# Mixer B's values leave PSUM through ScalarE alone, inverse roots in eight operations, and the first head's transposes behind a gate's matmuls

## The chip, the core and the metric

The kernel runs on one core of one Trainium2 chip. A core has TensorE (PE in the profile), VectorE (DVE), ScalarE (ACT), GpSimd (POOL) and SyncE (SP, which only issues DMAs). The metric is the device time of one execution in microseconds (us); smaller is better.

## The reference

Two layers of an encoder trunk on x of 512 tokens by 1024 channels, all in float32. Each layer has two attention branches whose outputs are gated, added and projected, and then a feed-forward part with a short convolution. The part of one layer that matters here:

```python
h = rms_norm(x, norm_mix[l])
z = h @ w_in[l]
qa, ka, va, qi, ki, wi, cq, ckv, kr, ga, gb = split_cols(z)
y_a = sparse_indexed_attention(qa, ka, va, qi, ki, wi, rel_bias, topk)  # topk = 128

cq = rms_norm(cq, b_cq_norm[l])                      # 384 wide
qb = (cq @ b_w_uq[l]).reshape(B, S, 8, 96)           # 64 plain + 32 rotated
ckv = rms_norm(ckv, b_ckv_norm[l])                   # 256 wide
kv = (ckv @ b_w_ukv[l]).reshape(B, S, 8, 64 + 64)    # keys | values
kb = concat([kv[..., :64], k_rope]);  vb = kv[..., 64:]
qb = rms_norm(qb, b_q_norm[l]);  kb = rms_norm(kb, b_k_norm[l])
y_b = latent_attention(qb, kb, vb)                   # 8 heads, softmax, chunk mask

merged = sigmoid(ga + ..) * (y_a @ w_proj_a[l]) + sigmoid(gb + ..) * (y_b @ w_proj_b[l])
x = x + merged @ w_out[l]
```

`rms_norm` is x times the inverse square root of mean(x²) + 1e-6, times a gain.

## The kernel before

**Matmuls.** Every float32 operand is split into a high part (`..h`, rounded) and a low part (`..l`, the rest), and each product is three matmuls (high·high, low·high, high·low) that add up in one PSUM bank of 128 x 512. A weight arrives by DMA as `wr`; ScalarE casts it to `wh`; and `wl` = `wr` − `wh` comes either from VectorE, or from ScalarE and a DMA that GpSimd issues. PSUM has eight banks: two `D` (dense products), three `L` (small products and scores), two `T` (transposes), one `Y` (attention outputs).

**Order of a layer.** Norm, index scores of mixer A, the latent rows, the gate columns `gb` m = 0 to 3; then `attn_b(0)` and `attn_b(1)`, which make keys, queries and values of heads 0 to 3 and 4 to 7; then mixer B head by head; then mixer A, the output projections, and the feed-forward part. What is dense (`gb` m = 4 to 7, gate A, projections) is written as a `Filler` from which a `Feeder` takes a step now and then, so that TensorE has matmuls between the steps of the heads. `top_k` (16 rounds, on VectorE alone, of three `MAX` and three `MATCH_REPLACE` over 512, 384 and 256 columns) is taken in the same way. The order in which the code is written gives each instruction a priority; a scheduler then sets each engine's final order by priorities and its own costs. On the chip each engine runs its own list strictly in that order and waits at semaphores.

**What attn_b does.** For each of four row tiles t, six matmuls (L846) make 128 x 512 in an `L` bank, with the keys of four heads in columns 0 to 255 and the values in columns 256 to 511. ScalarE copies the keys to `kn` (L852) and casts the values to the high half of `vb` (L313, in `split_into`); VectorE subtracts that from the PSUM bank for the low half (L314); ScalarE squares the keys into `sqb` (L833), which VectorE sums to `ssk` (L834). The bank is free when all four are done. The queries go in the same way (nine matmuls L883, copy L889 to `qn`, squares, `ssq`), and GpSimd rotates 32 of each head's 96 columns. Behind the tiles `keys()` and `queries()` (L860, L908) work out inverse roots `y` with `rsqrt` and scale `kn` (L870) and `qn` (L914) with them on VectorE.

**What a head of mixer B does.** `turn_b(h)` transposes the head's columns of `qn` (four transposes into one `T` bank, L1139) and of `kn` (four more into the other); each bank is then cast to `tbh` by ScalarE and its low part `tbl` is made by VectorE (L314 for queries, L317 for keys, which have a gain). The bank is free when both have read it. `scores_b(h)` multiplies them in three matmuls for each row tile (L1154 to L1156), VectorE finds the row maximum (L1157), ScalarE takes the exponential into `P`, VectorE normalizes (L1046, L1053), and `values` transposes `P` (L1064) and multiplies it with `vb` (L1071). The steps of head h, the values of head h−1 and the transposes of head h+1 are woven.

**The root.** `rsqrt(a)` makes a first guess from the bits of `a` (L345) and then three Newton steps of three VectorE operations each (L354 to L356): ten operations on 128 x 4 or 128 x 16. There are 22 calls in the program. The norms copy the result to `rstd` with one more.

Of the kernel before, what the change touches and what calls it, by code (L numbers as in the profile page):

```python
# [15 lines left out]
OP = mybir.AluOpType  # L16
AX = mybir.AxisListType
# [7 lines left out]
EPS = 1e-6  # L25
# [53 lines left out]
LAG_D = [2, 4, 5, 7, 8, 10, 12]  # L79
WPOOL = []  # L80
WMOD = 1
NEWT = 1
WB = [4, 4, 3]
ENDS = 20
SPARE = (1, 3, 5)
# [7 lines left out]
GB_0 = 4  # L93
GB_1 = 4
GAP_I = 4
GAP_A = 12
BB = 'L'
LAG_N = 16
# [147 lines left out]
def trunk(ctx: ExitStack, tc: tile.TileContext, xT, wd, vecs, bias, rot_n, outT):  # L246
# [92 lines left out]
        mm(p, lhsT=ah, rhs=bl, start=False, stop=False, skip_group_check=True)  # L339
        mm(p, lhsT=al, rhs=bh, start=False, stop=stop, skip_group_check=True)  # L340

    def rsqrt(a, shape, quick=False):

        y, t = small("y", shape), small("t", shape)
        V.tensor_scalar(y.bitcast(I32), a.bitcast(I32), -0.5, float(0x5F3759DF), op0=OP.mult, op1=OP.add)  # L345
        if not (quick or NEWT):
            for _ in range(3):
                G.tensor_tensor(out=t, in0=y, in1=y, op=OP.mult)
                G.tensor_tensor(out=t, in0=t, in1=a, op=OP.mult)
                G.tensor_scalar(t, t, -0.5, 1.5, op0=OP.mult, op1=OP.add)  # L350
                G.tensor_tensor(out=y, in0=y, in1=t, op=OP.mult)
            return y
        for _ in range(3):
            V.tensor_tensor(out=t, in0=y, in1=y, op=OP.mult)  # L354
            V.scalar_tensor_tensor(t, t, -0.5, a, op0=OP.mult, op1=OP.mult)
            V.scalar_tensor_tensor(y, t, 1.5, y, op0=OP.add, op1=OP.mult)  # L356
        return y

    def pin(ins, i, k):
        if i == 0 and k in PINS:  # L360
# [89 lines left out]
    class Norm:  # L450
# [17 lines left out]
        def finish(self, gap):  # L468

            p = bank("T")  # L470
            for i in range(4):
                pin(mm(p[:, i:i + 1], lhsT=self.acc[:, i * 128:(i + 1) * 128], rhs=ones[:, 0:1], start=True,
                       stop=True), i, "F")
            v = small("v", [4])
            self.epsv = cst.tile([128, 4], F32, name=nm("epsv"))
            self.rstd = cst.tile([128, 4], F32, name=nm("rstd"))
            V.tensor_scalar(v, p[:, 0:4], 1.0 / D, EPS, op0=OP.mult, op1=OP.add)
            r = rsqrt(v, [4], quick=True)
            V.tensor_copy(self.rstd, r)
            V.tensor_scalar(self.epsv, v, EPS, None, op0=OP.mult)  # L480
            self.row = slot("row")

            def rest():
                self.spread(self.rstd, self.row)
                for f in self.waiting:
                    f()
                self.waiting = None
            later(gap, rest)
# [76 lines left out]
    def mix_dense(l, nrm):  # L565
# [23 lines left out]
        def turn_wk(wk):  # L589
            p = bank("T")  # L590
            for i in range(4):
                nc.tensor.transpose(p[:, i * 40:(i + 1) * 40], wk[64:104, i * 128:(i + 1) * 128],
                                    ident[64:104, 64:104])
            wn = slot("wn")
            A.copy(wn[:, 0:160], p[:, 0:160])
            n = wn[:, 0:160].rearrange("p (t c) -> p t c", c=40)

            w4 = slot("w4")
            iw = w4[:, 0:32].rearrange("p (t h) -> p t h", h=8)
            ia = w4[:, 32:64].rearrange("p (t h) -> p t h", h=8)  # L600
            sg = w4[:, 64:96].rearrange("p (t h) -> p t h", h=8)
            r2 = small("r2", [4])
            V.scalar_tensor_tensor(r2, nrm.rstd, IDX_SCALE, nrm.rstd, op0=OP.mult, op1=OP.mult)
            G.tensor_tensor(out=iw, in0=n[:, :, 32:40], in1=r2[:, :, None].to_broadcast([128, 4, 8]), op=OP.mult)
            G.tensor_scalar(sg, iw, 0.0, 2.0, op0=OP.is_ge, op1=OP.mult)
            G.tensor_scalar(sg, sg, -1.0, None, op0=OP.add)
            G.tensor_tensor(out=ia, in0=iw, in1=sg, op=OP.mult)
            st["ia"], st["sg"] = ia, sg
            done.add("idx")

            cos = rotn[:, 0:64].rearrange("p (t c) -> p t c", c=16)
            sin = rotn[:, 64:128].rearrange("p (t c) -> p t c", c=16)
            kr = slot("kr")
            k3 = kr[:, 0:128].rearrange("p (t c) -> p t c", c=32)
            t3 = kr[:, 128:256].rearrange("p (t c) -> p t c", c=32)
            x1, x2 = n[:, :, 0:16], n[:, :, 16:32]
            G.tensor_tensor(out=k3[:, :, 0:16], in0=x1, in1=cos, op=OP.mult)
            G.tensor_tensor(out=t3[:, :, 0:16], in0=x2, in1=sin, op=OP.mult)
            G.tensor_tensor(out=k3[:, :, 16:32], in0=x1, in1=sin, op=OP.mult)
            G.tensor_tensor(out=t3[:, :, 16:32], in0=x2, in1=cos, op=OP.mult)  # L620
            G.tensor_tensor(out=k3[:, :, 0:16], in0=k3[:, :, 0:16], in1=t3[:, :, 0:16], op=OP.subtract)
            G.tensor_tensor(out=k3[:, :, 16:32], in0=k3[:, :, 16:32], in1=t3[:, :, 16:32], op=OP.add)
            G.tensor_tensor(out=k3, in0=k3, in1=nrm.rstd[:, :, None].to_broadcast([128, 4, 32]), op=OP.mult)
            G.tensor_tensor(out=t3, in0=k3, in1=k3, op=OP.mult)
            ss = cst.tile([128, 4], F32, name=nm("sskr"))
            later(6, lambda: V.tensor_reduce(out=ss, in_=t3, axis=AX.X, op=OP.add))
            st["kr"], st["sskr"] = k3, ss

        raw, sqs = [], []
# [193 lines left out]
        def attn_b(g):  # L823
# [15 lines left out]
            for t in range(4):  # L839
# [11 lines left out]
                p = p.rearrange("p (h c) -> p h c", c=64)  # L851
                A.copy(k4[t][:, :, 0:64], p[:, 0:4])  # L852
                v = vb[t].rearrange("p (h c) -> p h c", c=128)
                split_into(v[:, :, 0:64], v[:, :, 64:128], p[:, 4:8])
                squares(p[:, 0:4], ssk[:, t], 64)
                yield

            def keys():
                m = small("mk", [4, 4])
                V.tensor_tensor(out=m, in0=ssk, in1=st["sskr"][:, :, None].to_broadcast([128, 4, 4]), op=OP.add)  # L860
                V.tensor_scalar(m, m, 1.0 / 96, EPS, op0=OP.mult, op1=OP.add)
                r = rsqrt(m, [4, 4])

                def scale():
                    for t in range(4):
                        G.tensor_tensor(out=k4[t][:, :, 64:96],
                                        in0=st["kr"][:, t:t + 1, :].to_broadcast([128, 4, 32]),
                                        in1=r[:, t, :, None].to_broadcast([128, 4, 32]), op=OP.mult)
                        G.tensor_copy(k4[t][:, :, 96:100], late_k[:, t:t + 1, :].to_broadcast([128, 4, 4]))
                        (G if "K" in POOL else V).tensor_tensor(out=k4[t][:, :, 0:64], in0=k4[t][:, :, 0:64],  # L870
                                        in1=r[:, t, :, None].to_broadcast([128, 4, 64]), op=OP.mult)
                later(LAG_S, scale)
# [258 lines left out]
    def turn_b(h):  # L1131
# [4 lines left out]
        for x, gain in ((qn, None), (kn, gab[0:100, 2 * st["l"] + 1:2 * st["l"] + 2])):  # L1136
            p = bank("T")
            for t in range(4):
                pin(nc.tensor.transpose(p[0:100, t * 128:(t + 1) * 128], x[t][:, c], ident), t, "B")  # L1139
            hi, low = slot("tbh", F32R), slot("tbl", F32R)  # L1140
            split_into(hi[0:100], low[0:100], p[0:100], gain)
            d += [hi, low]
# [498 lines left out]
```

## Time and profile before

| | |
|---|---|
| runs | 1539.43, 1538.64, 1540.41 us; median 1539.43 |
| profiled execution | 1539.65 us, its span 1537.9 us, granted TensorE clock 1.00 |
| PE busy | 1528.4 us, 99% of the span |
| DVE, ACT, POOL busy | 73%, 62%, 26% |
| mixer B and what leads to it, layer 0 | about 84 to 170 us |
| the same, layer 1 | about 860 to 940 us |

The profile is of one execution. Its rows give start and duration of each instruction; matmuls overlap their neighbours, so that a matmul's cost is the distance between two starts and not its duration. A row's bracket, where there is one, gives the idle time of the engine before it and what ended it.

### The profile page before, as it was taken

The page shows a single profiled execution, that of the slowest core. Times are in us where ns is not written, and L with a number is a line of the kernel's source. Part 1 is how long each engine was busy: PE and PEld are TensorE (multiplying, and loading weights), DVE is VectorE, ACT ScalarE, POOL GpSimd, SP SyncE. Part 2 cuts the span into 40 slices and gives each one's busy share as a digit, 9 for nine tenths or more (in the row PEclk, how much of TensorE's full clock was granted, in tenths as well). Part 3 has the DMA queues.
Part 4 walks back from the last instruction along what each step waited for, and adds up shares of the span by engine and source line. Part 5 has one row for each costly group of instructions (what it writes and reads, how often), then busy time and mean ns, then how long its engine had stood idle before and what let it go on. Part 6 is the DMA issues. An engine that isn't in the chain of part 4 may idle for free.

```text
span 1537.9 us, 23961 instructions
## 1 busy us (share of the span) xinstructions
PE 1528.4 (99%) x8666; PEld 1337.2 (87%) x8666; DVE 1124.1 (73%) x2303; ACT 946.2 (62%) x1553; POOL 396.4 (26%) x578
## 2 busy tenths in 40 slices
PE   9999999999999999999999999999999999999999
PEld 8887999888888898889998889998888888988899
DVE  7899988666476793548979999886574857835587
ACT  7756677773577536664557577686635765456642
POOL 2343013400012331224602520224001115311264
PEclk9999999999999999999999999999999999999999
DMA  6464134733477448873554641356435783588733
GB/s 244 102 162 123 45 95 110 188 117 120 126 189 184 110 117 218 196 176 90 157 166 112 157 109 56 104 131 172 130 97 148 179 186 95 149 200 193 176 95 100
DMA packets 73575, 216.29 MB, mean 141 GB/s; under 512 B 8432, under 2 KB 11504, under 8 KB 73456
## 3 DMA queue, kind: packets, MB, share of 16 engines
q1 hardware_dynamic: 54592, 149.08, 30.8%
q0 software_dynamic: 18432, 65.28, 22.7%
q8 instruction: 68, 1.11, 0.3%
q14 instruction: 51, 0.42, 0.1%
q10 hardware_dynamic: 432, 0.40, 0.1%
HBM read 141.06 MB, written 4.19 MB: 94 GB/s over the span
## 4 chain that ended last, share of the span: by engine, by line
PE 85%; DVE 10%; ACT 3%; issue 1%; POOL 0%; ACTq 0%; DVEq 0%
PE D L528 36%; PE T L528 15%; PE D L551 7%; PE L L1436 5%; PE T L1436 4%; PE D L1436 3%; PE Y L1071 2%; DVE sc L1033 2%; PE Y L1436 2%; DVE m L1026 2%; PE T L1064 2%; PE L L528 2%; PE L L335 1%; PE L L334 1%; PE L L718 1%
## 5 line engine op out<-in xcount | busy, mean ns | idle before, releaser
L181 ACT CAST wh<-wr 128x1024 fp32r<-128x1024 f32 (+2 forms) x205 | 211.3, 1034 | 164.7 <-PE D L528 73.8
L210 POOL DMA_DIRECT2D wl<-wr x128 | 110.8, 875 | 635.5 <-ACT wl L209 596.1
L528 PE MATMUL D<-hxh,wh 128*128 128x512 f32 (+1 forms) x440 | 174.1, 396 | 0.0
L528 PE MATMUL D<-hxl,wh 128*128 128x512 f32 (+1 forms) x440 | 172.9, 393 | 0.0
L209 ACT ACTIVATE wl<-wr 128x1024 fp32r<-128x1024 f32 (+2 forms) x128 | 132.1, 1035 | 47.9 <-PE D L528 25.7
L199 ACT CAST wh<-wr 128x896 fp32r<-128x896 f32 x88 | 82.6, 941 | 101.3 <-POOL wr L223 51.6
L1105 POOL TENSOR_TENSOR P<-M,sel 128x128 f32<-128x128 f32 (+1 forms) x64 | 54.5, 906 | 269.8 <-DMA M<-in_bias_dram 133.2
L528 PE MATMUL D<-hxh,wl 128*128 128x512 f32 (+1 forms) x440 | 117.9, 394 | 0.0
L551 PE MATMUL D<-wh,hxh 128*128 128x256 f32 x384 | 113.7, 297 | 0.0
L223 POOL TENSOR_TENSOR wr<-wr 128x256 f32<-128x256 f32 x88 | 95.3, 1086 | 60.6 <-DVE wr L222 51.2
L551 PE MATMUL D<-wl,hxh 128*128 128x256 f32 x384 | 109.3, 285 | 0.0
L551 PE MATMUL D<-wh,hxl 128*128 128x256 f32 x384 | 108.5, 283 | 0.0
L204 DVE TENSOR_TENSOR wl<-wr,wh 128x896 fp32r<-128x896 f32 x88 | 103.8, 1183 | 5.8 <-ACT wh L199 3.1
L193 DVE TENSOR_TENSOR wl<-wr,wh 128x1024 fp32r<-128x1024 f32 x77 | 95.1, 1241 | 7.1 <-ACT wh L181 5.9
L528 PE MATMUL D<-hrl,wh 128*128 128x512 f32 x256 | 99.6, 389 | 0.0
L528 PE MATMUL D<-hrh,wh 128*128 128x512 f32 x256 | 99.6, 389 | 0.0
L528 PE MATMUL T<-hrh,wh 128*128 128x512 f32 x256 | 99.6, 389 | 0.0
L528 PE MATMUL T<-hrl,wh 128*128 128x512 f32 x256 | 99.6, 389 | 0.0
L528 PEld LDWEIGHTS D<-hxh,wh 128*128 128x128 f32 x440 | 82.9, 188 | 13.4 <-DVE gb L692 0.2
L528 PEld LDWEIGHTS D<-hxl,wh 128*128 128x128 f32 x440 | 82.9, 188 | 12.7
L528 PEld LDWEIGHTS D<-hxh,wl 128*128 128x128 f32 x440 | 80.2, 188 | 14.0
L1380 DVE SCALAR_TENSOR_TENSOR c<-T,vec,c 128x511 f32<-128x511 f32 x32 | 23.9, 747 | 89.1 <-ACT c L1377 89.1
(454 smaller groups left out, 4578.2 us busy)
## 6 DMA issues: line engine op xcount, KB each, us to landing
wr<-in_wd_dram SPq DMA_DIRECT2D x197, 512.0 KB, 3.7
wl<-wr POOLq DMA_DIRECT2D x120, 512.0 KB, 5.3
wr<-in_wd_dram SPq DMA_DIRECT2D x88, 256.0 KB, 2.7
x<-in_xT_dram SPq DMA_DIRECT2D x16, 256.0 KB, 5.0
M<-in_bias_dram SPq DMA_DIRECT2D x16, 256.0 KB, 4.0
wr<-in_wd_dram SPq DMA_DIRECT2D x7, 384.0 KB, 3.3
kah<-kah SPq DMA_DIRECT2D x16, 128.0 KB, 4.3
kal<-kal SPq DMA_DIRECT2D x16, 128.0 KB, 3.6
```

The costliest lines, as they stand in the source:

```text
L181: ins = self.nc.scalar.copy(h[:, :n], t[:, :n])
L193: eng.tensor_tensor(out=o[:, c], in0=t[:, c], in1=h[:, c].bitcast(F32), op=OP.subtract)
L199: self.nc.scalar.copy(h[:, :896], t[:, 128:1024])
L204: self.later(lag, lambda: self.nc.vector.tensor_tensor(out=o[:, :896], in0=t[:, 128:1024], in1=h[:, :896].bitcast(F32), op=OP.subtract))
L209: self.nc.scalar.activation(o, t, AF.Copy, scale=-1.0)
L210: self.nc.gpsimd.dma_start(o.bitcast(F32), t, accum_op=OP.add)
L223: g(2)(out=b[:, 6:8], in0=b[:, 0:3:2], in1=b[:, 3:6:2], op=OP.add)
L528: mm(p[:, t0:], lhsT=w, rhs=x[:, t0:], start=n == 0, stop=n == len(seq) - 1, skip_group_check=True)
L551: mm(pp[b][:, t, :], lhsT=x, rhs=w, start=n == 0 and half == 0 and t == 0, stop=n == 11 and half == 1, skip_group_check=True)
L1026: ins = V.max(out=m8[i], in_=st["sc"][i][:, :128 * (i + 1)])
L1105: G.tensor_tensor(out=P[:, P0[i]:P0[i] + w], in0=M[:, 512 - w:512], in1=sel[:, SEL0[i]:SEL0[i] + w], op=OP.add)
L1436: mm(p, lhsT=w, rhs=x, start=b0, stop=b1, skip_group_check=True)
```

## The change

1. In `attn_b` the values are first copied by ScalarE from the `L` bank to a slot `vr` in SBUF (one slot for two row tiles). The cast to the high half of `vb` and VectorE's subtraction read `vr` and no longer the bank. ScalarE has 16 instructions more.
2. `rsqrt` makes one Newton step and then one cubic step: eight VectorE operations in place of ten, at all 22 calls. The norms write `rstd` with the last operation (four copies fewer). In `keys()` two operations become one (four fewer), since `sskr` is scaled ahead, once for a layer, by GpSimd (two instructions more there).
3. The transposes of head 0 are put down by 160 places in priority.

```diff
-NEWT = 1
+CUBE = 0.375 ** 0.5
+LATE_B = 160
...
-    def rsqrt(a, shape, quick=False):
+    def rsqrt(a, shape, out=None):
         y, t = small("y", shape), small("t", shape)
         V.tensor_scalar(y.bitcast(I32), a.bitcast(I32), -0.5, float(0x5F3759DF), op0=OP.mult, op1=OP.add)
...
-        for _ in range(3):
-            V.tensor_tensor(out=t, in0=y, in1=y, op=OP.mult)
-            V.scalar_tensor_tensor(t, t, -0.5, a, op0=OP.mult, op1=OP.mult)
-            V.scalar_tensor_tensor(y, t, 1.5, y, op0=OP.add, op1=OP.mult)
-        return y
+        V.tensor_tensor(out=t, in0=y, in1=y, op=OP.mult)
+        V.scalar_tensor_tensor(t, t, -0.5, a, op0=OP.mult, op1=OP.mult)
+        V.scalar_tensor_tensor(y, t, 1.5, y, op0=OP.add, op1=OP.mult)
+        V.tensor_tensor(out=t, in0=y, in1=y, op=OP.mult)
+        V.scalar_tensor_tensor(t, t, -CUBE, a, op0=OP.mult, op1=OP.mult)
+        V.scalar_tensor_tensor(t, t, 1.25 / CUBE, t, op0=OP.add, op1=OP.mult)
+        V.scalar_tensor_tensor(y if out is None else out, t, 1.875, y, op0=OP.add, op1=OP.mult)
+        return y if out is None else out
...
-            r = rsqrt(v, [4], quick=True)
-            V.tensor_copy(self.rstd, r)
+            rsqrt(v, [4], self.rstd)
...
-            later(6, lambda: V.tensor_reduce(out=ss, in_=t3, axis=AX.X, op=OP.add))
+            def key_sums():
+                V.tensor_reduce(out=ss, in_=t3, axis=AX.X, op=OP.add)
+                G.tensor_scalar(ss, ss, 1.0 / 96, EPS, op0=OP.mult, op1=OP.add)
+            later(6, key_sums)
...
                 v = vb[t].rearrange("p (h c) -> p h c", c=128)
-                split_into(v[:, :, 0:64], v[:, :, 64:128], p[:, 4:8])
+                if t % 2 == 0:
+                    vr = slot("vr")
+                raw = vr[:, t % 2 * 256:t % 2 * 256 + 256].rearrange("p (h c) -> p h c", c=64)
+                A.copy(raw, p[:, 4:8])
+                split_into(v[:, :, 0:64], v[:, :, 64:128], raw)
                 squares(p[:, 0:4], ssk[:, t], 64)
...
-                V.tensor_tensor(out=m, in0=ssk, in1=st["sskr"][:, :, None].to_broadcast([128, 4, 4]), op=OP.add)
-                V.tensor_scalar(m, m, 1.0 / 96, EPS, op0=OP.mult, op1=OP.add)
+                V.scalar_tensor_tensor(m, ssk, 1.0 / 96, st["sskr"][:, :, None].to_broadcast([128, 4, 4]),
+                                       op0=OP.mult, op1=OP.add)
...
             for t in range(4):
-                pin(nc.tensor.transpose(p[0:100, t * 128:(t + 1) * 128], x[t][:, c], ident), t, "B")
+                with tc.high_priority(offset=-LATE_B) if h == 0 else ExitStack():
+                    nc.tensor.transpose(p[0:100, t * 128:(t + 1) * 128], x[t][:, c], ident)
```

The scheduler answers with another order in three places that matter, shown for layer 0; layer 1 has the same pattern. The numbers in the names count tiles and differ between the two kernels.

TensorE, between the last query matmuls of `attn_b(1)` and the first scores. Before, head 0's transposes (`qn_180` is row tile 0 of the queries, `kn_176` of the keys) stand early among the matmuls of gate column m = 4 (`D_279`, weights `wh20`, `wl20`), and head 1's query transposes (`T_266`) come after four of its eight `wl20` matmuls:

```order
L528 MATMUL D_279_1560<-hxh_35_182,wh20_1237 128x512
L1139 MATMUL T_253_1429<-ident_117,qn_180_1057 100x128 [waits DVE_49]
L1139 MATMUL T_258_1452<-ident_117,kn_176_1053 100x128 [waits Pool_49]
...
L1139 MATMUL T_253_1429<-ident_117,qn_183_1060 100x128 [waits DVE_49]
L528 MATMUL D_279_1560<-hxh_41_194,wh20_1237 128x512
...
L528 MATMUL D_279_1560<-hxh_31_174,wl20_1238 128x512
L1139 MATMUL T_266_1479<-ident_117,qn_180_1057 100x128 [waits DVE_49]
```

After, on the same engine, all 16 `wh20` and five `wl20` matmuls stand ahead of head 0's transposes, and the next gate column (`D_306`, m = 5) has begun between those and head 1's (`T_270`):

```order
L524 MATMUL D_283_1560<-hxh_35_182,wl20_1237 128x512
L1144 MATMUL T_257_1429<-ident_117,qn_180_1053 100x128 [waits DVE_49]
...
L1144 MATMUL T_257_1429<-ident_117,qn_183_1056 100x128 [waits DVE_49]
...
L524 MATMUL D_306_1668<-hxh_17_146,wh21_1337 128x512
L1144 MATMUL T_262_1452<-ident_117,kn_176_1049 100x128
...
L524 MATMUL D_306_1668<-hxl_26_163,wh21_1337 128x512
L1144 MATMUL T_270_1479<-ident_117,qn_180_1053 100x128 [waits DVE_49]
```

Counted over the two gate columns, 28 dense matmuls stand ahead of head 1's query transposes in place of 20 (layer 1: 35 in place of 21). Those transposes reuse the bank of head 0's, so the wait on VectorE there is for head 0's `tbl`.

VectorE, around that `tbl` of head 0's queries, before (`sc_..`, `m8_..` belong to top-k; `y`, `t` to the keys' root of `attn_b(1)`):

```order
L914 TENSOR_TENSOR qn_183_1060<-qn_183_1060,y_231_1292 128x4x96
L354 TENSOR_TENSOR t_244_1381<-y_243_1380 128x16
L834 TENSOR_REDUCE ssq_226_1271<-sqb_239_1360 128x4
L355 SCALAR_TENSOR_TENSOR t_244_1381<-t_244_1381,mk_242_1377 128x16
L1033 MATCH_REPLACE sc_108_645<-m8_164_874,sc_108_645 128x384
L356 SCALAR_TENSOR_TENSOR y_243_1380<-t_244_1381,y_243_1380 128x16
L314 TENSOR_TENSOR tbl_255_1435<-T_253_1429,tbh_254_1434 100x512
L354 TENSOR_TENSOR t_244_1381<-y_243_1380 128x16
L1033 MATCH_REPLACE sc_134_752<-m8_163_873,sc_134_752 128x256
```

And after, where the root is finished first and more of top-k stands ahead:

```order
L350 TENSOR_TENSOR t_248_1383<-y_247_1382 128x16
L1030 MAX m8_163_869<-sc_134_748 128x8
L351 SCALAR_TENSOR_TENSOR t_248_1383<-t_248_1383,mk_246_1380 128x16
L1037 MATCH_REPLACE sc_88_555<-m8_165_871,sc_88_555 128x512
L352 SCALAR_TENSOR_TENSOR t_248_1383<-t_248_1383 128x16
L1037 MATCH_REPLACE sc_108_643<-m8_164_870,sc_108_643 128x384
L353 SCALAR_TENSOR_TENSOR y_247_1382<-t_248_1383,y_247_1382 128x16
L315 TENSOR_TENSOR tbl_259_1435<-T_257_1429,tbh_258_1434 100x512
L874 TENSOR_TENSOR kn_215_1257<-kn_215_1257,y_247_1382 128x4x64
```

Counted on VectorE from the evacuation of gate column m = 3 to this `tbl`: in layer 0, one `MATCH_REPLACE` more of each width, three `MAX` more (one of each width) and two small operations fewer; in layer 1, one `MATCH_REPLACE` more of each width, two `MAX` more, four scalings of `kn` more and three small operations fewer.

ScalarE, at the values of `attn_b(1)`'s first row tile, before:

```order
L852 COPY kn_213_1258<-L_227_1272 128x4x64
L313 CAST vb_221_1266<-L_227_1272 128x4x64
L833 ACTIVATE sqb_228_1283<-L_227_1272 128x256
L852 COPY kn_214_1259<-L_229_1286 128x4x64
```

After, where the cast reads what the copy ahead of it wrote, and the bank's last reader is the square:

```order
L852 COPY kn_215_1257<-L_229_1271 128x4x64
L857 COPY vr_230_1281<-L_229_1271 128x256
L314 CAST vb_223_1265<-vr_230_1281 128x4x64
L833 ACTIVATE sqb_231_1284<-L_229_1271 128x256
```

More of the change, by code (lines that the diff above doesn't have):

```diff
@@ L340, in mm3 @@
         mm(p, lhsT=al, rhs=bh, start=False, stop=stop, skip_group_check=True)
-    def rsqrt(a, shape, quick=False):
+    def rsqrt(a, shape, out=None):
         y, t = small("y", shape), small("t", shape)
         V.tensor_scalar(y.bitcast(I32), a.bitcast(I32), -0.5, float(0x5F3759DF), op0=OP.mult, op1=OP.add)
-        if not (quick or NEWT):
-            for _ in range(3):
[L348 to L351, printed above, removed]
-            return y
-        for _ in range(3):
-            V.tensor_tensor(out=t, in0=y, in1=y, op=OP.mult)
-            V.scalar_tensor_tensor(t, t, -0.5, a, op0=OP.mult, op1=OP.mult)
-            V.scalar_tensor_tensor(y, t, 1.5, y, op0=OP.add, op1=OP.mult)
-        return y
+        V.tensor_tensor(out=t, in0=y, in1=y, op=OP.mult)
[6 more added lines that the diff above has]
+        return y if out is None else out
     def pin(ins, i, k):
```

## Prediction, made before the changed kernel ran

> **What bounds the kernel now.** I read the page's busy times first, then what TensorE waits for, then the busy time of each engine by stage, and last the rows around the waits.
>
> ```profile
> span 1537.9 us, 23961 instructions
> PE 1528.4 (99%) x8666; PEld 1337.2 (87%) x8666; DVE 1124.1 (73%) x2303; ACT 946.2 (62%) x1553; POOL 396.4 (26%) x578
> ```
>
> TensorE works for 99% of the span. Nothing in the change takes a matmul away, so it can only gain what TensorE loses waiting, and only lose by new waits. The waits of the whole run that the change can touch:
>
> ```profile
> PE L L846 <- DVE vb L314: 1.2, 3, 0.6
> PE L L1154 <- ACT P L368: 0.6, 1, 0.6
> PE L L883 <- DVE vb L314: 0.5, 1, 0.5
> PE T L1139 <- DVE qn L914: 0.2, 1, 0.2
> ```
>
> They are small: four waits of a PSUM bank for VectorE's subtraction, 1.7 us idle, and one of head 0's transposes. All lie in two stretches:
>
> ```profile
> 84.00:113.00 29.00, 27.71 (x128) 22.80 (x127) 29.00 (x96) 18.12 (x41) 14.69 (x45) 1.00 0.65 154
> 113.00:135.00 22.00, 21.26 (x113) 16.82 (x111) 21.74 (x75) 16.03 (x34) 14.76 (x36) 1.00 0.54 124
> 860.00:880.00 20.00, 19.41 (x98) 16.60 (x96) 20.00 (x74) 15.49 (x36) 14.70 (x44) 1.00 0.76 184
> 880.00:903.00 23.00, 22.61 (x122) 17.99 (x120) 23.00 (x73) 18.00 (x36) 12.31 (x31) 1.00 0.56 121
> ```
>
> The columns after the length are busy time of PE, PEld, DVE, ACT, POOL. The third says it: VectorE is busy for 29.00 of 29.00, 21.74 of 22.00, 20.00 of 20.00 and 23.00 of 23.00 us, because top-k fills every hole. So here the place of an operation in VectorE's list decides when it runs, and TensorE has under 1.3 us of slack in any of these stretches.
>
> **What the copy by ScalarE removes.** TensorE at the bank waits:
>
> ```profile
> 95.47 0.39 PE L846 MATMUL L<-wl,ckvh 128*128 128x512 f32 x1
> 96.08 0.50 PE L846 MATMUL L<-wh,ckvh 128*128 128x512 f32 x1 [0.22 <-DVE vb L314]
> 96.42 0.40 PE L846 MATMUL L<-wh,ckvl 128*128 128x512 f32 x1
> ...
> 100.37 0.69 PE L883 MATMUL L<-wl,cqh 128*128 128x384 f32 x3
> 101.54 0.44 PE L883 MATMUL L<-wh,cqh 128*128 128x384 f32 x1 [0.48 <-DVE vb L314]
> ...
> 109.34 0.40 PE L528 MATMUL D<-hxl,wh 128*128 128x512 f32 x1
> 110.31 0.49 PE L846 MATMUL L<-wh,ckvh 128*128 128x512 f32 x1 [0.58 <-DVE vb L314]
> ...
> 872.78 0.39 PE L528 MATMUL D<-hxh,wh 128*128 128x512 f32 x1
> 873.59 0.50 PE L846 MATMUL L<-wh,ckvh 128*128 128x512 f32 x1 [0.42 <-DVE vb L314]
> ```
>
> Undisturbed, matmuls of 512 columns start 0.23 us apart and those of 384 0.17 us. The steps over the waits are 0.61, 1.17 (three matmuls of 384 first), 0.97 and 0.81 us, so the waits cost 0.38, 1.17 − 3 x 0.17 = 0.66, 0.74 and 0.58 us, and 0.11 us more at the slow second matmul (96.08 to 96.42 is 0.34). Layer 0 loses 2.1 us, layer 1 0.7 us. Afterwards the bank is read by ScalarE alone: a copy, a copy, a cast, a square. Such operations start 0.26 us apart:
>
> ```profile
> 99.08 0.35 ACT L852 COPY kn<-L 128x256 f32<-128x256 f32 x1
> 99.33 0.38 ACT L313 CAST vb<-L 128x256 fp32r<-128x256 f32 x1
> ```
>
> With a fourth, and a wait for the copy ahead of the cast, the square ends some 1.35 us after the first copy starts. A tile's six matmuls take 6 x 0.23 = 1.38 us and there are three banks, so ScalarE keeps up, even with a weight cast of about 1 us between. I take all of it: −2.1 and −0.7 us. Bounds: 0 if ScalarE becomes the late one, −2.8 together.
>
> The copies' own price is 16 x 0.26 = 4.2 us of ScalarE, hidden by its idle time (18.12 of 29.00 us busy); without that cover it would be paid in full. VectorE's subtraction has the same shape, and now reads SBUF twice. Its nearest row is the scaling of `kn`, with two inputs in SBUF:
>
> ```profile
> L314 DVE TENSOR_TENSOR vb<-L,vb 128x256 fp32r<-128x256 f32 x8 | 3.3, 411 | 0.0
> L870 DVE TENSOR_TENSOR kn<-kn,y 128x256 f32<-128x256 f32 x8 | 3.1, 412 | 0.0
> ```
>
> 411 ns from PSUM, 412 ns from SBUF: I take no change. [...]
>
> **What the later transposes do.** Before, head 0's query transposes wait for `qn`, and head 1's follow early:
>
> ```profile
> 116.75 0.38 PE L1139 MATMUL T<-ident,kn 128*100 128x128 f32 x2
> 117.28 0.32 PE L1139 MATMUL T<-ident,qn 128*100 128x128 f32 x1
> ...
> 120.64 0.60 PE L1139 MATMUL T<-ident,qn 128*100 128x128 f32 x4
> ...
> 878.92 0.39 PE L528 MATMUL D<-hxh,wh 128*128 128x512 f32 x1
> 879.48 0.32 PE L1139 MATMUL T<-ident,qn 128*100 128x128 f32 x1 [0.17 <-DVE qn L914]
> ...
> 883.89 0.64 PE L1139 MATMUL T<-ident,qn 128*100 128x128 f32 x4
> ```
>
> With dense matmuls ahead the waits for `qn` go. Transposes start 0.11 us apart, so the step to 117.28 holds 0.53 − 0.22 = 0.31 us of waiting; with two smaller ones behind it I take 0.5 in layer 0. In layer 1 it is 0.56 − 0.23 = 0.33 us.
>
> The bill comes at head 1's query transposes. They reuse head 0's bank, and so wait for VectorE's `tbl`:
>
> ```profile
> 119.74 0.68 DVE L314 TENSOR_TENSOR tbl<-T,tbh 100x512 fp32r<-100x512 f32 x1
> ...
> 883.16 0.68 DVE L314 TENSOR_TENSOR tbl<-T,tbh 100x512 fp32r<-100x512 f32 x1
> ...
> 114.75 0.67 DVE L1033 MATCH_REPLACE8 sc<-m,sc 128x512 f32<-128x512 f32 x1
> 115.35 0.41 DVE L314 TENSOR_TENSOR vb<-L,vb 128x256 fp32r<-128x256 f32 x1
> ...
> L1026 DVE MAX8 m<-sc x96: 398/548/695, 53.9 to 931.3; 128x8 f32<-128x512 f32 x32, 128x8 f32<-128x384 f32 x32, 128x8 f32<-128x256 f32 x32
> L1033 DVE MATCH_REPLACE8 sc<-m,sc x96: 397/541/678, 54.7 to 936.9; 128x512 f32<-128x512 f32 x32, 128x384 f32<-128x384 f32 x32, 128x256 f32<-128x256 f32 x32
> ...
> L354 DVE TENSOR_TENSOR t<-y 128x16 f32<-128x16 f32 x12 | 2.4, 199 | 0.0
> ```
>
> The two group rows give shortest, middle and longest, which are the widths 256, 384 and 512. An operation overlaps the next by 0.07 to 0.08 (114.75 + 0.67 against 115.35), so the three `MAX` cost 0.33, 0.47 and 0.61, 1.4 together; a replace costs its duration, as a load of 0.07 precedes it, 1.6 for the three; scaling `kn` 0.33; a small operation 0.20 − 0.07 = 0.13. By the counts under the change, layer 0 has 1.6 + 1.4 − 2 x 0.13 = 2.7 us more ahead of `tbl`: it starts at 122.4 and ends at 123.1. TensorE would come to it at 120.64 − 2.1 − 0.5 + 8 x 0.23 = 119.9 and so waits 3.2 us. The eight dense matmuls ahead are work done: against 120.64 + 1.84 = 122.5, TensorE is 0.6 us late. In layer 1: 1.6 + 1.1 + 4 x 0.33 − 3 x 0.13 = 3.6 more, `tbl` ends at 883.16 + 3.6 + 0.68 = 887.4; against 883.89 + 14 x 0.23 = 887.1 that is 0.3 us late, after a wait of 1.3 us. All that the first two terms brought is gone in this wait, since VectorE and not TensorE sets when head 1 goes on. Bounds of the two together: from −3.6 (no wait at all) to +3 (a second round of top-k, 3.0 us, ahead of `tbl`, in one layer).
>
> Behind it: VectorE's round is then done already, so the next late thing moves less.
>
> ```profile
> 133.22 0.39 PE L528 MATMUL D<-hxl,wh 128*128 128x512 f32 x1
> 134.16 0.50 PE L1154 MATMUL L<-tbh,tbh 100*128 100x512 f32 x1 [0.56 <-ACT P L368]
> ...
> 136.62 0.68 DVE L692 TENSOR_TENSOR gb<-D,row 128x512 f32<-128x512 f32 x1
> ```
>
> The step to 134.16 costs 0.94 − 0.23 = 0.7 us; TensorE, coming later, meets less of it (−0.4 taken of 0 to −0.7). The evacuation of gate column m = 4, at 136.62, stands behind the same VectorE list and comes later; a dense matmul of the next column waits for that bank: +0.3 in each layer, between 0 and +1.5.
>
> **Roots.** In the two stretches eight to ten small operations a layer go, about 0.13 us each, 1.2 us: VectorE is full, so that top-k moves up by as much, and it is in the counts above as far as it precedes `tbl`. The norms' roots (outside these stretches) save three operations of about 0.2 us each at four places; in the waits of the whole run the only one that a norm could own is under 0.3 us. Taken at nothing, −0.5 at best. GpSimd's two operations: nothing.
>
> **Sum**, by the state behind head 1's transposes, where the first terms are already in: layer 0 +0.6 − 0.4 + 0.3 = +0.5; layer 1 +0.3 + 0.3 = +0.6; together +1.1, less 0.3 for top-k ending a little sooner (between 0 and −1.2 in each layer). So +0.8 us. The profiled execution, 1539.65 us (span 1537.9 and 1.75 around it), lies 0.22 above the median; in terms of runs, 1539.43 + 0.8 = 1540.2. A measurement of this kernel cannot tell less than 0.2%, 3.1 us, from no change.
>
> **Rivals.**
>
> Faster: VectorE paces, and what leaves it counts. If `tbl` comes 3 us earlier than I reckon, the wait at head 1 does not arise and the removed waits stay: −2.1 − 0.7 − 0.5 − 0.3 = −3.6 us, and with some of top-k's gain −4. For it speaks that VectorE's list was full in every window; against it, that the order puts a whole round ahead of `tbl` where TensorE has no other bank. It gives 1535.5.
>
> Slower: the subtraction now has both inputs in SBUF and is held up by GpSimd. One such operation was, in this trace:
>
> ```profile
> L908 DVE SCALAR_TENSOR_TENSOR mq<-ssq,ms x4: 157/382/1266, 110.2 to 895.8; 128x16 f32<-128x16 f32 x4
> ```
>
> 1.27 us for what takes 0.16 alone, while GpSimd rotated queries. Five of a layer's eight subtractions fall among such rotations; each hold passes to `tbl` and so to TensorE. From a mean hold of 0.25 us the kernel is slower by over 3.1 (10 x 0.25 = 2.5, and 0.8); with 0.3 it is 1543.2. Against it stands the scaling of `kn` quoted above, 412 ns on the mean with two SBUF inputs. [...]
>
> Without effect: the waits that go were not on the path, or the scheduler's round is caught up with at once. Then 1539.4, within my own range.
>
> **How the numbers follow.** Forecast 0.47 (1538.2 to 1542.2), without effect 0.08, faster rival 0.28, slower 0.17. Some of the faster rival stops short of 3.1 us and some of the forecast's tail lies beyond it; they even out. So faster by over 0.2%: 0.28, within 0.2%: 0.55, slower: 0.17. The range takes in both rivals' times: 1535.0 to 1543.5.
>
> **What would show it.** In the profile after: no wait of `L` banks for `vb`; no wait of head 0's transposes for `qn`; in their place a wait of head 1's query transposes (L1144) for `tbl` of 2 to 3.5 us in layer 0 and 1 to 2 in layer 1; `tbl` of head 0 at about 122.5 and 886.7 us; `vb` subtractions of 0.41 us. It is wrong if that wait is missing (then faster), or if the subtractions read over 0.6 us (then slower).

## The result: 12 us slower

The changed kernel takes 1551.26 us (median of six runs, 1550.09 to 1552.28) and the kernel before 1539.33 (six runs): a ratio of 1.0074, interval 1.0063 to 1.0085. The forecast was 1540.2, range 1535.0 to 1543.5. The profiled execution after took 1550.09 us, the lowest of its six. From its page, span and busy times, and from the list of TensorE's waits (us in total, times, longest):

```profile
span 1548.4 us, 23932 instructions
PE 1529.1 (99%) x8666; PEld 1339.7 (87%) x8666; DVE 1119.5 (72%) x2251; ACT 952.1 (61%) x1569; POOL 397.7 (26%) x580
...
PE T L1144 <- DVE tbl L315: 7.2, 2, 4.0
PE T L1144 <- DVE qn L918: 1.3, 3, 0.8
...
PE Y L1075 <- DVE ptl L315: 1.2, 1, 1.2
```

Fewer VectorE operations and the same matmuls, yet 10.5 us more span. The bank waits for `vb` are gone, as forecast. In their place stand two waits of head 1's query transposes for `tbl`, 7.2 us where 4.5 were forecast. The waits for `qn`, which were to go, are longer: 1.3 us where the whole run before had 0.2, all of them at head 0's transposes in layer 0. The same two stretches after, by stage (busy time of PE, PEld, DVE, ACT, POOL, then the granted clock):

```profile
84.00:113.00 29.00, 29.00 (x141) 25.29 (x140) 29.00 (x85) 22.15 (x52) 15.53 (x46) 1.00 0.64 153
113.00:135.00 22.00, 17.51 (x94) 13.91 (x94) 21.80 (x70) 12.19 (x27) 12.29 (x35) 1.00 0.49 121
860.00:880.00 20.00, 20.00 (x101) 17.74 (x100) 20.00 (x65) 18.98 (x48) 14.66 (x44) 1.00 0.69 165
880.00:903.00 23.00, 18.99 (x92) 16.58 (x91) 21.31 (x63) 12.08 (x23) 11.70 (x29) 0.85 0.49 119
```

TensorE is never idle in the first stage of each pair (29.00, 20.00), and gives it all back in the second: 17.51 of 22.00, where before it had 21.26. VectorE is as full as it was, but for the last stage (21.31 of 23.00). And in the last row the clock is 0.85, which nothing in the prediction had.

Set side by side, the same dense matmuls run 2.9 us later than before once layer 0's mixer B is through, keep that distance to 855 us, are 9.0 late at 908 and 10.0 at 960; in mixer A of layer 1 they go from 9.9 at 1015 to 11.1 at 1030, and are 10.4 late from 1060 to the end (times of the kernel before).

Layer 0, VectorE's and then GpSimd's rows (start, duration):

```profile
108.78 2.70 DVE L874 TENSOR_TENSOR kn<-kn,y 128x256 f32<-128x256 f32 x1
...
111.86 0.41 DVE L874 TENSOR_TENSOR kn<-kn,y 128x256 f32<-128x256 f32 x1
...
124.31 0.68 DVE L315 TENSOR_TENSOR tbl<-T,tbh 100x512 fp32r<-100x512 f32 x1
```

```profile
107.36 0.98 POOL L900 TENSOR_TENSOR rot<-qn,rotn 128x64 f32<-128x64 f32 x1
...
108.46 0.49 POOL L870 TENSOR_TENSOR kn<-kr,y 128x128 f32<-128x128 f32 x1
108.82 0.41 POOL L902 TENSOR_TENSOR qn<-qn,rotn 128x64 f32<-128x64 f32 x1
...
110.29 0.82 POOL L870 TENSOR_TENSOR kn<-kr,y 128x128 f32<-128x128 f32 x2
111.00 0.91 POOL L873 COPY kn<-latek 128x16 f32<-128x16 f32 x4
```

One scaling of `kn` takes 2.70 us in place of 0.41, and ends when GpSimd's run without a gap (107.36 to 111.91) nears its end. `tbl` comes at 124.31 (forecast 122.4, before 119.74). Of `vb` no row is that long; the sixteen subtractions, shortest, middle and longest:

```profile
L315 DVE TENSOR_TENSOR vb<-vr,vb x16: 398/412/637, 96.3 to 883.4; 128x256 fp32r<-128x256 f32 x16
```

Layer 1, VectorE and then TensorE's two long waits:

```profile
889.94 2.13 DVE L874 TENSOR_TENSOR kn<-kn,y 128x256 f32<-128x256 f32 x4
892.00 0.68 DVE L315 TENSOR_TENSOR tbl<-T,tbh 100x512 fp32r<-100x512 f32 x1
```

```profile
125.04 0.64 PE L1144 MATMUL T<-ident,qn 128*100 128x128 f32 x4 [3.16 <-DVE tbl L315]
892.73 1.09 PE L1144 MATMUL T<-ident,qn 128*100 128x128 f32 x4 [4.01 <-DVE tbl L315]
```

The four transposes take 0.64 us in layer 0 and 1.09 in layer 1: there they run on half the clock (granted 0.50 from 891.57 to 898.40 us).

### The profile page after: what moved, and what is told of

The parts are those of the page before. It is cut to its first block, busy times and chain, and to the rows that moved or that the text cites. A ratio compares the mean times of both kernels' runs of the same rounds, so it can differ in the third digit from the quotient of the medians.

```text
span 1548.4 us, 23932 instructions
## 1 busy us (share of the span) xinstructions
PE 1529.1 (99%) x8666; PEld 1339.7 (87%) x8666; DVE 1119.5 (72%) x2251; ACT 952.1 (61%) x1569; POOL 397.7 (26%) x580
## 4 chain that ended last, share of the span: by engine, by line
PE 86%; DVE 11%; ACT 2%; issue 1%; POOL 0%; DMA 0%; SPq 0%; ACTq 0%; DVEq 0%
PE D L524 36%; PE T L524 15%; PE D L547 7%; PE L L1441 5%; PE T L1441 4%; PE D L1441 3%; PE Y L1075 3%; DVE sc L1037 2%; DVE m L1030 2%; PE T L1068 2%; PE Y L1441 2%; PE L L524 2%; PE L L335 1%; PE L L336 1%; PE L L718 1%
```

## The experiments

In the expectations, theory A is that the place of operations in VectorE's list around `tbl` costs the 12 us, theory B that GpSimd holds VectorE's operations that have two inputs in SBUF, and C that the copy costs by itself. "Over before" is the difference of medians in runs on the same chip.

### Which part

**The change without the later transposes:**

```diff
-LATE_B = 160
+LATE_B = 0
```

> The changed kernel with head 0's transposes back at their usual priority (values' copy and eight-operation roots stay). Theory A: the later transposes alone cost the 12 us, because in VectorE's list a round of top-k (and in layer 1 the scaling of kn) gets ahead of head 0's tbl. In this kernel 23 and 22 operations of top-k stand ahead of tbl since gate column m = 3 in place of 28 and 28, so the waits of head 1's query transposes for tbl go, the clock stays 1.00, and the removed bank waits stay: 1536 to 1539 us. Theory B: the subtraction with two inputs in SBUF is held up by GpSimd and costs most of it: 1546 us or more.

1547.89 us, ratio 1.0052 (1.0035 to 1.0068).

**The kernel before with only the later transposes** (`LATE_B = 160` and the `high_priority` line of the change).

> The kernel before with nothing but head 0's transposes put down by 160. Theory A: 25 and 26 operations of top-k ahead of tbl in place of 22 and 23, roots in ten operations as before; waits for tbl of 2 to 4 us in both layers, 1543 to 1552 us. Theory B: within 2 us of before, 1538 to 1541 us.

1541.18 us, 1.0012 (1.0002 to 1.0021).

**The kernel before with only the new root** (part 2 of the change).

> The kernel before with the eight-operation roots, the rstd copies gone and the fused key mean, and nothing else. Both theories: little, 1537.5 to 1540 us; the saved small operations of VectorE go to top-k.

1543.15 us, 1.0026 (1.0015 to 1.0037).

**The kernel before with only the values through ScalarE** (part 1).

> The kernel before with nothing but the values' copy by ScalarE. Theory A: the four bank waits for vb (2.8 us with what hangs on them) go and no long wait comes: 1536 to 1539 us. Theory B: subtractions held by GpSimd, 1544 us or more.

1546.02 us, 1.0042 (1.0026 to 1.0058). TensorE's waits, of no_late, then late_alone, then values_alone:

```profile
PE T L1144 <- DVE qn L918: 7.9, 2, 4.7
```

```profile
PE L L1157 <- DVE tbl L318: 1.3, 2, 0.7
PE T L1141 <- DVE tbl L315: 1.0, 2, 0.6
```

```profile
PE T L1143 <- DVE qn L918: 8.3, 2, 5.0
```

Theory A as put falls: the later transposes alone cost 1.8 us, and without them the change still loses 8.5. B's numbers fit for no_late and values_alone, and late_alone is at the edge (1538 to 1541 expected). roots_alone, for which both expected 1537.5 to 1540, fits neither. The three parts add up to 6.6 + 3.8 + 1.8 = 12.2 over before, against 11.9 for the whole; that is partly chance, since the first two together (no_late) cost 8.5 and not 10.4. The largest is the one that removes waits. With the values out of the banks early TensorE runs ahead, and stands at the next thing that VectorE owes: at `qn` for 8.3 us where the transposes are early, at `tbl` where they are late.

### GpSimd's holds

In values_alone, VectorE and GpSimd:

```profile
114.13 1.95 DVE L356 SCALAR_TENSOR_TENSOR y<-t,y 128x16 f32<-128x16 f32 x1
```

```profile
113.94 0.59 POOL L900 TENSOR_TENSOR rot<-qn,rotn 128x64 f32<-128x64 f32 x1
...
115.86 0.28 POOL L906 COPY qn<-lateq 128x16 f32<-128x16 f32 x1
```

A root's operation of 0.16 us takes 1.95, to the end of GpSimd's run. From the evacuation of gate column m = 3 to head 0's `tbl`, the operations on 128 x 16 (the roots and the small sums ahead of them), each counted from its start to the next start, took 3.83 us in layer 0 and 3.57 in layer 1 before, and 6.32 and 5.82 here. Of these, 1.02 and 1.06 us are no holds: VectorE is idle there ahead of `tbl`, until ScalarE's `tbh` is written.

**The kernel before, and values_alone, without the rotation.** The six GpSimd multiplications and additions that rotate a query tile are left out, so that part of the queries is not rotated; before_norot has before's order on VectorE.

```diff
-                    G.tensor_tensor(out=w[0], in0=x1, in1=b(sin), op=OP.mult)
-                    ...
-                    G.tensor_tensor(out=x2, in0=x2, in1=w[0], op=OP.add)
```

> The kernel before without the six GpSimd instructions that rotate each query tile (the rotation of mixer B's queries is left out of the computation), everything else in the same order on VectorE. It is the base for values_norot. Theory B (VectorE operations with two SBUF inputs wait for runs of GpSimd instructions) and theory C (what hurts is ScalarE's extra work and VectorE's late list, not GpSimd) both expect little: 1536 to 1540 us.

> The values' copy alone, again without the rotation of mixer B's queries on GpSimd. Theory B: with the runs of GpSimd instructions gone, the holds of the roots and of kn go, the removed bank waits remain as a gain, and it is 0 to 3 us faster than before_norot. Theory C: it stays slower than before_norot by about what values_alone is slower than before, 4 to 7 us.

before_norot 1535.63 us, 0.9977 (0.9968 to 0.9987): the same list, 3.9 us sooner, the roots at 2.56 and 2.57 us. So the kernel before paid for holds too. These operations give 2.3 of the 3.9 us; whether the rest is holds as well, or queries that are ready sooner without the rotation, this run does not tell. values_norot 1540.29, 1.0007 (0.9997 to 1.0016): 4.7 over its own base, with the roots at 2.88 and 3.14. B had expected it at or below its base, C 4 to 7 us above it, and C's number came. Holds by the rotation are therefore not all of the price of the copy. Its waits:

```profile
PE T L1135 <- DVE qn L910: 2.5, 1, 2.5
PE Y L1067 <- DVE ptl L314: 1.5, 1, 1.5
PE T L1135 <- DVE mk L864: 1.5, 1, 1.5
```

The first and the third are head 0's transposes, to which TensorE comes early. The second lies in mixer A of layer 1, at another GpSimd run; of values_norot, VectorE and GpSimd:

```profile
1018.94 0.84 DVE L354 TENSOR_TENSOR t<-y 128x16 f32<-128x16 f32 x1
1019.82 1.08 DVE L355 SCALAR_TENSOR_TENSOR t<-t,m 128x16 f32<-128x16 f32 x1
```

```profile
1017.81 3.05 POOL L1101 TENSOR_TENSOR P<-M,sel 128x128 f32<-128x128 f32 x4 [8.10 <-DMA M<-in_bias_dram]
```

In the kernel before, these two operations take 0.18 and 0.17 us, and the run follows them, released by the root (1019.44). Later operations of the same root are long beside it, but TensorE then waits only 0.2 us at `Y`:

```profile
1019.92 0.61 DVE L354 TENSOR_TENSOR t<-y 128x16 f32<-128x16 f32 x1
...
1021.45 1.08 DVE L356 SCALAR_TENSOR_TENSOR y<-t,y 128x16 f32<-128x16 f32 x1
```

In values_norot the bias `M` released the run first, and the first operations of the root fall inside. They fall inside in the changed kernel too, where the run starts at 1027.51 and two of them take 0.84 and 1.08 us; its wait of 1.2 us at `Y` follows. values_alone, with the roots of before, waits 1.4 us there.

**The values copied, the subtraction reading the bank as before:**

```diff
-                split_into(v[:, :, 0:64], v[:, :, 64:128], raw)
+                A.copy(v[:, :, 0:64], raw)
+                later(1, lambda v=v, p=p: V.tensor_tensor(out=v[:, :, 64:128], in0=p[:, 4:8],
+                                 in1=v[:, :, 0:64].bitcast(F32), op=OP.subtract))
```

> The values' copy alone, but VectorE's subtraction still takes its first input from the PSUM bank; ScalarE has the 16 extra copies and the cast reads the copy. Theory B: one SBUF input, so no more is held than before, the bank waits for vb stay: 1538.5 to 1541 us. Theory C (ScalarE's extra copies make kn, vb and the squares late): 1543 us or more.

1542.59 us, 1.0022 (1.0012 to 1.0031), between the two expectations. The roots take 3.86 and 3.81 us, nearly as before, and the bank waits are back, so TensorE does not run ahead. The profile is of the fastest of its ten executions (1540.78; the others go up to 1545.30 at the same clock), so it does not show what makes the median 3.05 us longer than before.

### The list around tbl

**The changed kernel with top-k's rounds from 13 on, and the scaling of heads 4 to 7's `kn`, made to follow head 0's `tbl`** (the comments are added here):

```diff
+                if rnd == HOLD:          # 12, counted from 0
+                    behind(ins)          # tc.add_manual_dep(ins, tbl, no_sync)
```

> The changed kernel, with top-k from its 13th round on and the scaling of kn of heads 4 to 7 made to stand behind head 0's tbl in VectorE's list (23 and 21 operations of top-k ahead of tbl in place of 28 and 28). Theory A (the later transposes cost what the list puts ahead of tbl): 3 us earlier in layer 0, 4 to 5 in layer 1, no drop of the clock, 1539 to 1543 us. Theory B: the holds in the roots and kn come earlier than this place and stay, 1545 to 1549 us.

1543.19 us, 1.0025 (1.0014 to 1.0036), just above the 1539 to 1543 that A expected. It is 3.65 over before, so 8.3 of the 11.9 us come back, though A fell as the whole cause. The wait for `tbl`:

```profile
PE T L1155 <- DVE tbl L1161: 2.4, 2, 1.4
```

**The same with the subtraction reading the bank; late_alone with the hold; the kernel before with the hold:**

> The changed kernel with the late rounds of top-k and the scaling of kn held behind head 0's tbl (as in after_hold, 1543.2), and VectorE's subtraction for vb reading the PSUM bank again (the cast reads vr). Theory HELD (what is left of the loss, 3.7 us, is GpSimd holding the subtractions and what follows them): 1539.5-1541.5, though the L banks' waits for vb come back. Rival CHAIN (the extra step by ScalarE, or the shorter roots, cost it): 1542.5-1545.

> The kernel before with head 0's transposes lowered by 160 places and the late rounds of top-k and kn held behind tbl; values and roots as before. Theory ORDER (the lowered transposes lose only what VectorE's list puts ahead of tbl; late_alone was 1541.2): 1537.5-1539.8. Rival DENSE (they lose because dense matmuls are used up ahead of them): 1540.5-1542.

> The kernel before with nothing but the hold (late rounds of top-k and the scaling of kn of heads 4 to 7 behind head 0's tbl). A control for after_hold. Theory ORDER (before has that order already, within one MATCH_REPLACE): 1538-1541. Rival GENERAL (the hold would gain in any of these kernels, so that after_hold says nothing on the change): 1530-1536.

hold_psum 1543.47 us, 1.0030 (1.0020 to 1.0041); late_hold 1539.61, 0.9999 (0.9991 to 1.0008); before_hold 1540.01, 1.0001 (0.9992 to 1.0010). The control gains nothing, so the 8.3 us are the change's own; and the later transposes, once nothing is put ahead of `tbl`, cost nothing and bring nothing. In after_hold the scaling of `kn` in layer 0 is held as long as in the changed kernel (3.56 us for four, against 3.63), and yet the dense matmuls are only 0.5 us late behind layer 0's mixers, against 2.9: that hold costs its full time only where rounds of top-k stand ahead of `tbl` as well. In hold_psum the scaling of `kn` is held less (1.82 us), and the roots more (5.42 and 6.42 us, against 3.46 and 4.65); but 1.06 and 1.42 us of that are VectorE's idle time until `tbh` is written, and the bank waits for `vb` are back at 3.9 us. There the holds became fewer, and what they no longer cost came back as other waits: theory HELD falls, and its rival's number came. No version with the whole computation beats the kernel before.

### The clock

**The changed kernel with twelve more transposes into the `Y` bank**, in layer 1 among the dense matmuls ahead of head 1's query transposes, read by nobody:

```diff
+            if gain is None and h == 1 and st["l"] == 1:
+                y = bank("Y")
+                with tc.high_priority(offset=-LATE_B):
+                    for j in range(12):
+                        last = nc.tensor.transpose(y[0:100, ...], qn[j % 4][:, c], ident)
```

> The changed kernel with twelve transposes more on TensorE (into the free Y bank, read by nobody) between the dense matmuls ahead of head 1's query transposes in layer 1; VectorE's list ahead of that tbl is unchanged. They shorten TensorE's pause there from 4.0 to about 2.7 us, and do no useful work. Theory CLOCK (a pause of 4.0 us lowers the granted clock to 0.50 for some 6 us and costs 3.3 us on top of the wait, one of 3.2 us does not): the clock stays at 1.00 behind the pause, and the time falls from 1551.3 to 1547-1549 although TensorE has 1.3 us of work more. Rival END (the end of tbl alone sets the time; the lower clock hits matmuls that would wait anyway, or has another cause): 1550-1552.5, or the clock falls all the same.

1551.81 us, 1.0078 (1.0064 to 1.0092). The rival's number came, and the clock fell all the same. But as a test of the clock the run missed: the pause was not filled but moved, to the scores' wait for the keys' `tbl`.

```profile
PE L L1167 <- DVE tbl L318: 4.3, 1, 4.3
PE T L1149 <- DVE tbl L315: 3.2, 1, 3.2
```

It showed something else: in layer 0, whose list is the changed kernel's, the clock fell behind a pause of 3.15 us, where it had not behind 3.16.

**The changed kernel, two more executions:**

> The changed kernel once more, unchanged, for its profile. In its first profile TensorE paused 3.16 us in layer 0 with the granted clock at 1.00 behind it, and 4.01 us in layer 1 with the clock at 0.50 for 6.82 us. Theory WINDOW (the clock is decided at the ends of windows of 3.41 us that run on without regard to the program, by how much of the window TensorE stood still): the pauses are the same again within 0.1 us, and a lower clock, where there is one, lasts 3.41 or 6.82 us; in layer 0 it appears in some executions and not in others, in layer 1 nearly always. Rival LENGTH (a pause above a fixed length, between 3.16 and 4.0 us, starts it): layer 0 never, layer 1 always for 6.82 us.

> As for the second execution of the changed kernel: WINDOW has layer 0's clock fall in some executions and the low stretch at 3.41 or 6.82 us; LENGTH has layer 0 never lowered and layer 1 always by the same stretch.

1551.41 and 1549.41 us. Stretches of 3.41 us, laid at the points where the clock changed (and, in layer 0 of the first execution, at the same points moved back by 225 such stretches); busy time of PE is the first number behind the length, the clock the third from the end. First execution, second, third:

```profile
120.16:123.57 3.41, 1.73 (x10) 1.06 (x8) 3.41 (x15) 2.81 (x5) 0.00 (x0) 1.00 0.50 156
123.57:126.98 3.41, 1.94 (x12) 1.80 (x13) 3.41 (x12) 0.59 (x1) 2.51 (x3) 1.00 0.02 5
888.16:891.57 3.41, 0.56 (x3) 0.13 (x1) 3.41 (x13) 0.04 (x1) 2.07 (x5) 1.00 0.25 99
891.57:894.98 3.41, 2.25 (x9) 2.14 (x10) 3.18 (x7) 1.11 (x2) 2.55 (x9) 0.50 0.75 150
894.98:898.40 3.42, 3.42 (x14) 3.42 (x13) 2.00 (x7) 1.82 (x5) 0.04 (x1) 0.50 0.48 135
898.40:901.81 3.41, 3.41 (x24) 3.33 (x23) 3.37 (x10) 2.70 (x6) 1.82 (x7) 1.00 0.05 22
```

```profile
120.27:123.68 3.41, 0.78 (x5) 0.34 (x3) 3.41 (x15) 1.85 (x4) 0.06 (x1) 1.00 0.43 153
123.68:127.09 3.41, 2.89 (x10) 2.59 (x11) 3.41 (x8) 0.59 (x1) 3.41 (x5) 0.50 0.02 5
...
891.68:895.09 3.41, 0.86 (x7) 0.82 (x8) 3.41 (x8) 0.18 (x1) 3.41 (x11) 1.00 0.29 58
895.09:898.51 3.42, 3.42 (x14) 3.42 (x13) 3.07 (x9) 2.15 (x4) 0.53 (x3) 0.50 0.65 115
```

```profile
121.34:124.75 3.41, 0.67 (x5) 0.67 (x6) 3.41 (x14) 0.67 (x2) 1.25 (x1) 1.00 0.07 25
124.75:128.16 3.41, 3.41 (x12) 3.16 (x12) 2.72 (x7) 0.59 (x1) 3.41 (x8) 0.50 0.10 20
```

The same program pauses 3.15 to 3.16 us in layer 0 each time, and the clock falls in two executions of three. So not the length alone decides but where the pause lies: a stretch in which TensorE was busy for 0.56 to 0.86 of 3.41 us is followed by one at half clock, stretches with 1.73 and 1.94 are not. In fill12 it was 1.19 and 1.23, and the clock fell:

```profile
122.26:125.67 3.41, 1.19 (x8) 1.06 (x8) 3.41 (x13) 0.65 (x2) 1.76 (x1) 1.00 0.04 11
125.67:129.08 3.41, 3.41 (x13) 3.41 (x12) 2.63 (x8) 0.08 (x1) 3.41 (x10) 0.50 0.20 40
...
890.27:893.68 3.41, 1.23 (x9) 0.90 (x7) 3.41 (x11) 0.65 (x1) 2.69 (x6) 1.00 0.00 1
```

In the third execution the clock falls in layer 1 too, for one stretch, behind one with 0.00 us of TensorE. Six of the 16 profiles show falls, 11 in all, and the stretch at full clock ahead of each has between 0.00 and 1.23 us of busy time; the other ten executions have a granted clock of 1.000. Laid through the first execution, the grid has 0.56 us ahead of the fall and 1.73 or more in every other stretch at full clock that ends before TensorE's last matmul, each followed by full clock; none lies between.

Half clock lasted one stretch where TensorE was busy for 2.89 us or more of it, and two where it was busy for 2.25 (2.23 in no_late, 1.30 in fill12). In each execution that shows both, the points lie a whole number of stretches apart (895.09 − 123.68 is 226 of 3.4133 us). Theory WINDOW stands. Counted as half lost, the busy time at half clock costs (2.25 + 3.42) / 2 = 2.8 us in the first execution and (2.89 + 3.42) / 2 = 3.2 in the second, an estimate. For one such fall there is a direct measure: from layer 0's transposes (125.04, 124.20 and 124.08) to the evacuation of gate column m = 3 in layer 1 the executions take 734.75, 736.29 and 736.22 us, 1.5 more where the clock fell.

```profile
859.79 0.66 DVE L692 TENSOR_TENSOR gb<-D,row 128x512 f32<-128x512 f32 x1
```

```profile
860.49 0.67 DVE L692 TENSOR_TENSOR gb<-D,row 128x512 f32<-128x512 f32 x1
```

```profile
860.30 0.66 DVE L692 TENSOR_TENSOR gb<-D,row 128x512 f32<-128x512 f32 x1
```

The pauses of values_alone (5.0 and 3.3 us) and no_late (4.7 and 3.2) end with half clock as well, 3.41 to 6.83 us of it; in the profiled executions of late_alone, roots_alone, after_hold, psum_sub, hold_psum and values_norot (longest pause 2.5) there is none. In other executions of hold_psum there is: the five with a granted clock of 1.000 took 1541.94 to 1543.65 us, the three with 0.998 or 0.999 took 1545.21 to 1547.16. By the same estimate, half of TensorE's busy time at half clock (2.98 and 3.41 us), values_alone pays 3.2 us to the clock in its profiled execution. That one is the slowest of its four (1548.61, 9.2 over before), so 6.0 are left; the two with a granted clock of 0.999 took 1543.90 and 1544.73, 4.5 and 5.3 over. The copy thus costs more than its falls of the clock do.

## Why the prediction was wrong

**Right.** The bank waits went, head 1's transposes got a wait for `tbl` in their place, and what the first two terms brought was lost in it: "VectorE and not TensorE sets when head 1 goes on". The wait there in layer 0 is 3.2 us, as forecast, but by luck: both sides of it came 2 us late (TensorE at 121.9 and not 119.9, 1.3 of it for the waits for `qn` that were to go). The three `MAX` and three `MATCH_REPLACE` more cost 1.4 and 1.6 us in layer 0, to the digit. The subtraction's price was right: 412 ns in the middle from SBUF, a mean of 411 from PSUM before.

**Step 1 that failed: `tbl` at +2.7 and +3.6 us.** From the evacuation of m = 3 it came 4.4 and 5.6 us later (30.60 against 26.16, and 32.21 against 26.60). In layer 0 the scaling of `kn` is 2.3 longer, less 0.6 that the roots give beyond the count. In layer 1 the scaling adds 2.2 where the forecast had 1.3, `vb` 0.5 where it had none, and the roots 0.3 where they were to give 0.4. That is 1.7 us over the forecast in layer 0 and 2.0 in layer 1, and the long rows in it stand beside GpSimd's runs. That GpSimd causes them is shown on the lists of before and values_alone, not on this one, of which no run left the rotation out. The prediction had such holds as a rival at 0.17, with nearly the right size (a mean of 0.3 us for ten subtractions, 3.0; 3.7 came) but on the wrong operations: it set against them the scaling of `kn` in the kernel before, 412 ns on the mean, and took that row to speak for what the change would meet. A mean of 412 ns over eight said only that in that order `kn` met no run.

**Step 2: no term for the clock.** A wait of 3.2 us was forecast, as a wait. The waits of 3.2 and 4.0 us that came cost another 2.8 to 3.2 us behind them, by the estimate above. In the stretches of 3.41 us above, up to 1.23 us of busy time, matmuls and transposes (fill12), did not keep the clock up; 1.73 us did (the first execution).

**Step 3: the roots, "Taken at nothing".** Alone they cost 3.8 us. The profiled execution, 4.6 over that of before, loses 1.5 of them in mixer A of layer 0, where operations lie beside GpSimd's `P<-M,sel`, and 1.5 in layer 1; no run took the roots apart, so that cause is argued and not shown. Such a collision, 1.2 us in mixer A of layer 1 (9.9 late to 11.1), is in the changed kernel and was not forecast; as values_alone has it too, it needs no new roots.

**The ledger** against the profiled execution: forecast +0.8; the holds ahead of `tbl` 1.7 and 2.0; the clock 2.8; mixer A 1.2, of which 0.7 comes back behind it. That is 7.8 of the 10.4 us by which it is late; 2.6 us are not assigned. Some 0.4 of them may be the forecast's gain at the scores' wait for `P`, which did not come (0.7 us, against 0.6 before). The median run is 1.2 us above the profiled one; a fall of the clock in layer 0 (1.5 us), which that execution was spared, would explain it, and the six executions agree: three with a granted clock of 0.998 have the median 1550.79, three with 0.997 have 1552.04.

**What stays open.** That the rotation makes VectorE's operations longer is shown (before_norot: 2.56 and 2.57 us for the operations on 128 x 16, in place of 3.83 and 3.57). Which operation is held in a given order is not explained: in the kernel before, a scaling of `kn` at 110.26 us took 0.41 beside a busy GpSimd, and there it was GpSimd's own multiplication at 110.18 that took 0.69 in place of 0.32. The place in the list does not decide it alone: in layer 1 of the changed kernel the scalings of `kn` ahead of `tbl` took 3.64 us in the first execution and 5.76 in the second. Nor is it known what the copy of the values costs when neither a hold nor the clock is in play; values_norot's 4.7 us hold at least 1.5 of mixer A's collision and 1.2 in layer 0, and its three executions at a granted clock of 1.000 still took 1539.57 to 1540.29 us.

## What to carry to other kernels

A wait that is removed on one engine is worth something only if the engine it waited for gets ahead as well; where VectorE is full for the whole stage (29.00 of 29.00 us here), TensorE merely stands at the next thing VectorE owes, and one long pause was dearer than several short ones, since in 11 cases of 12 a pause of 3.15 to 5.0 us was followed by 3.41 or 6.83 us at half clock. Price a VectorE operation on SBUF that shares a stage with GpSimd by the longest row of any such operation (1.27 us for `mq` in the kernel before) and not by the mean of its own kind, since the mean belongs to the order in which it was measured. When a scheduler reorders around a change, first tie the order of the late operation down again and measure: here that gave back 8 of 12 us.

## What the runs showed of the hardware

- The half clock came and went in steps of 3.41 us, on a grid that lay elsewhere in each execution of the same program (points at 123.57, 123.68 and 124.75 us); up to 1.23 us of TensorE's busy time in the step before did not prevent it, 1.73 did.
- A VectorE operation beside a run of GpSimd without a gap lasted to the run's end or near it: 2.70 us in place of 0.41 (`kn`, the changed kernel), 1.95 in place of 0.16 (a root, values_alone). These two read two tiles in SBUF, and beside each stood a run of many instructions, not one. An operation with one such input was long beside a run as well: the root's first guess, at 1028.64 us of the changed kernel, took 0.84 us in place of 0.18.
- Leaving out GpSimd's rotation, with VectorE's list unchanged, took 3.9 us off the whole kernel, 2.3 of them at small operations of VectorE.
- In two executions of one program, VectorE's list the same, different operations were long: the scalings of `kn` ahead of layer 1's `tbl` took 3.64 and 5.76 us in all.
